# A hybrid-attention encoder layer on one core: sink logits as a score column, four rows normalized on ScalarE, one projection added by accumulating stores

## The chip, the cores and the metric

The kernel runs on one core of a Trainium2 chip. A core has TensorE (PE, matrix products into PSUM), VectorE (DVE), ScalarE (ACT) and GpSimd (POOL), and a queue on SyncE (SP) that issues DMA transfers; GpSimd issues transfers too. Each engine works through its own instructions in order and waits on semaphores for the others. The metric is the device time of one execution in microseconds, as a median over runs.

## The reference

One layer of a post-norm encoder on x of 1024 tokens by 1024 features, in float32:

```python
x = layer_norm(x, ln_in_g, ln_in_b)
proj = x @ w_in                                  # split into q, k, v of three groups
oa = neighbourhood_attention(...)                # A: 4 heads, 8x16 window on a 16x64 grid
ob = sliding_window_gqa(...)                     # B: 8 q heads, 2 kv heads, +-128 tokens, sinks
oc = differential_attention(...)                 # C: 4 heads, two softmaxes, full length
mix = concatenate([oa, ob, oc]) @ w_out
x = layer_norm(alpha * x + mix, ln_mix_g, ln_mix_b)
hdn = relu(x @ w_ff1)
x = layer_norm(alpha * x + (hdn * hdn) @ w_ff2, ln_ff_g, ln_ff_b)
```

In group B every query has one more logit, the sink of its head, which takes part in the softmax and has no value:

```python
sink_col = broadcast_to(sink, scores.shape[:-1] + (1,))
p = softmax(concatenate([scores, sink_col], axis=-1), axis=-1)[..., :-1]
```

## The kernel before

The 1024 tokens are eight tiles of 128. Products are made in two-part precision: each operand is split into a high part (a copy rounded to the matmul's type, on ScalarE) and a low part (a subtraction, L133, on VectorE or GpSimd), and `mm3` (L147) makes three products. Working tiles come from a pool of 36 pages of 4 KB per partition (`page`), and from small rings: `evb` has four buffers, PSUM has tags `S` (three banks), `mm` (two), `t` (two) and `pv` (one).

The program runs the input normalization and the first projections, then group C (steps 0 to 31 of one loop), group A (32 to 47), group B (48 to 63) with a few steps of lag for the values, and then the feed-forward layer, whose products (L930, L1044) fill TensorE to the end. Projections of later groups are put between as background work (`run_bg`). The order of instructions on each engine is set by a scheduler that simulates the program and follows priorities; `tc.high_priority(offset=...)` moves a block.

Group B is the third attention. One step `b_scores(i, g)` makes the scores of four heads for one tile of queries over up to three blocks of keys (n is 256 or 384 columns): for each head two matmuls (L720), one custom VectorE instruction (L722) that adds the position table, negates, writes the row to SBUF and gives the row's minimum against the negated sink, and one exponential on ScalarE (L725) whose accumulator gives the row's sum. Then four small instructions bring in the sinks: L728 adds sink and minimum (both in SBUF), L729 is its exponential, L730 adds the row sums (both in SBUF), L731 is the reciprocal. GpSimd multiplies the rows by it (L734). `b_values` transposes them (L746), splits them (L749, L133), multiplies by the values (L752) and splits the result (L755, L756, L761, L133 on 64x256).

`out_c(t)` makes group C's share of the output projection of tile t while groups A and B run, and stores its two halves to the DRAM tensor `y1c` from GpSimd's queue. `y1[t]` holds alpha times the normalized input, stored early. `out_ab(t, ob)` loads `y1[t]` and `y1c[t]` from SP's queue, adds them on GpSimd (L797), makes the shares of A and B (L147) and adds these on VectorE (L803). The eight results are normalized by `ln_mix_half`: statistics on VectorE (`ln_stats`, L210, L226, L228), a power on GpSimd (L229), the normalization itself on VectorE (L854), a store to `y2` from GpSimd's queue (L856), then transposes (L864) and splits. Half 0 (tiles 0 to 3) runs while group B still does, half 1 after it.

Of the kernel before, what the change touches and what calls it, by code (L numbers as in the profile page):

```python
# [13 lines left out]
AF = mybir.ActivationFunctionType  # L14
ALU = mybir.AluOpType
AX = mybir.AxisListType

P = 128
D = 1024
# [61 lines left out]
def encoder_kernel(ctx: ExitStack, tc: tile.TileContext, A: dict, out: bass.AP):  # L81
# [12 lines left out]
    def page(shape, dt=F32):  # L94
        return sb.tile(shape, dt, tag="pg", bufs=N_PG, name=nm("pg"))
# [25 lines left out]
    def dram(shape, name):  # L121
        return dr.tile(shape, F32, tag=name, bufs=1, name=name)
# [149 lines left out]
        return res  # L272

    y1 = [dram([P, D], f"y1_{t}") for t in range(NT)]
    y1c = dram([NT, P, D], "y1c")
    xT = [None, None]


# [429 lines left out]
    def b_scores(i, g, q, kk, tabs):  # L708
        k0, k1, off = b_range(i)
        n = (k1 - k0) * P  # L710
        sm = small([P, 4, 4], "bst")
        rts = []
        for h2 in range(2):
            rt = page([P, 2, 384])
            for j in range(2):
                hl = 2 * h2 + j
                sc = ps_s()
                h = 4 * g + hl
                for m in range(2):
                    nc.tensor.matmul(sc[:, 0:n], q[:, h, :], kk[g][m][:, k0 * P:k1 * P],  # L720
                                     start=(m == 0), stop=(m == 1))
                nc.vector.tensor_tensor_reduce(  # L722
                    out=rt[:, j, 0:n], in0=sc[:, 0:n], in1=tabs[h][:, off:off + n],
                    scale=-1.0, scalar=negsink[:, h:h + 1], op0=ALU.add, op1=ALU.min, accum_out=sm[:, 0, hl:hl + 1])
                nc.scalar.activation(out=rt[:, j, 0:n], in_=rt[:, j, 0:n], func=AF.Exp, scale=-1.0,  # L725
                                     bias=sm[:, 0, hl:hl + 1], accum_out=sm[:, 1, hl:hl + 1])
            rts.append(rt)
        nc.vector.tensor_tensor(out=sm[:, 2, :], in0=sink[:, 4 * g:4 * g + 4], in1=sm[:, 0, :], op=ALU.add)  # L728
        nc.scalar.activation(out=sm[:, 2, :], in_=sm[:, 2, :], func=AF.Exp)  # L729
        nc.vector.tensor_tensor(out=sm[:, 2, :], in0=sm[:, 2, :], in1=sm[:, 1, :], op=ALU.add)  # L730
        nc.vector.reciprocal(out=sm[:, 3, :], in_=sm[:, 2, :])  # L731
        for h2 in range(2):
            rt = rts[h2]
            nc.gpsimd.tensor_tensor(out=rt[:, :, 0:n], in0=rt[:, :, 0:n],  # L734
                                    in1=sm[:, 3, 2 * h2:2 * h2 + 2].unsqueeze(2).broadcast_to([P, 2, n]), op=ALU.mult)
        return rts
# [44 lines left out]
    def out_c(t):  # L781

        for nh in range(2):
            pm = ps_mm()
            sl = half_sl(nh)
            mm3(pm, [(*heads_of(t, n), w_o[6 + n][0][:, sl], w_o[6 + n][1][:, sl]) for n in range(2)])
            a_t = evb([P, 512])
            nc.scalar.copy(out=a_t, in_=pm)
            nc.gpsimd.dma_start(out=y1c[t, :, sl], in_=a_t)

    def out_ab(t, ob):

        a_t = page([P, D])
        load(out=a_t, in_=y1[t])
        c_t = page([P, D])
        load(out=c_t, in_=y1c[t])
        nc.gpsimd.tensor_tensor(out=a_t, in0=a_t, in1=c_t, op=ALU.add)  # L797
        for nh in range(2):
            pm = ps_mm()
            sl = half_sl(nh)  # L800
# [48 lines left out]
    def ln_mix_half(half):  # L849

        xs = fa[4 * half:4 * half + 4]
        for j in range(4):
            mean, rstd = ln_stats(xs[j])
            nc.vector.tensor_scalar(out=xs[j], in0=xs[j], scalar1=mean, scalar2=rstd,  # L854
                                    op0=ALU.subtract, op1=ALU.mult)
            nc.gpsimd.dma_start(out=y2[4 * half + j], in_=xs[j])  # L856
        if not ln_mix:
            ln_mix.append(ln_load("ln_mix"))
# [526 lines left out]
```

## Time and profile before

| what | us |
|---|---|
| median of 3 runs (1222.17 to 1224.81) | 1223.8 |
| the profiled execution | 1225.86 |
| its span in the profile | 1224.0 |
| TensorE, VectorE, ScalarE, GpSimd busy | 1148.0, 990.2, 642.9, 415.4 |

The span runs from the first to the last instruction of one profiled execution; times in the rows below count from its start. Busy time leaves out waits on semaphores, but not what an instruction waits for after it has begun. TensorE's ends are modelled, so its busy time is an upper figure. TensorE's mean granted clock is 0.98 of full speed.

### The profile page before, as it was taken

To read this page: it belongs to the slowest core of one execution; us is meant where nothing else is said; L and a number is where in the kernel's file an instruction comes from. 1 tells how busy PE (TensorE), PEld (TensorE's weight loads), DVE (VectorE), ACT (ScalarE), POOL (GpSimd) and SP (SyncE) were. 2 spreads that over 40 slices of the span, in tenths; PEclk is the share of its full clock that TensorE was granted. 3 is DMA by queue.
4 is the path that set the end of the run, shared out by engine and by line. 5 is a ranking of instruction groups with operands and counts; after the bars stand their busy time and mean duration, and the time that the engine had idled before them with its cause. 6 is when DMAs were issued, how large, how long until landed. Compare 5 with 4: busy or idle time off the path is not lost.

```text
span 1224.0 us, 17025 instructions
## 1 busy us (share of the span) xinstructions
PE 1148.0 (94%) x5642; PEld 949.4 (78%) x5642; DVE 990.2 (81%) x1886; ACT 642.9 (53%) x1239; POOL 415.4 (34%) x363
## 2 busy tenths in 40 slices
PE   4799999999998989988399999999999999999997
PEld 3578879987877867766288888888888888888886
DVE  7855899998666699986897698898684888777995
ACT  5323667766557876655655445455462444444440
POOL 5833556686576766531012122222120000000201
PEclk9889999999999999999599999999999999999999
DMA  7295835363789663324035575664389755255551
GB/s 237 104 303 162 276 127 167 121 166 123 209 228 303 199 164 104 104 86 155 26 129 180 175 244 191 225 230 154 141 318 346 250 178 190 103 187 189 183 163 69
DMA packets 127535, 220.59 MB, mean 180 GB/s; under 512 B 11404, under 2 KB 67628, under 8 KB 127448
## 3 DMA queue, kind: packets, MB, share of 16 engines
q1 hardware_dynamic: 113752, 173.36, 45.3%
q0 software_dynamic: 13696, 46.15, 9.9%
q8 instruction: 45, 0.74, 0.3%
q14 instruction: 42, 0.34, 0.1%
HBM read 152.30 MB, written 74.98 MB: 186 GB/s over the span
## 4 chain that ended last, share of the span: by engine, by line
PE 76%; DVE 12%; issue 5%; DMA 2%; ACT 2%; POOL 1%; SPq 0%; DVEq 0%; POOLq 0%; ACTq 0%
PE psm L147 15%; PE psS L1044 11%; PE psS L930 10%; PE pst L930 7%; PE psm L930 7%; PE pst L1044 5%; PE psm L1044 5%; PE pspv L1044 4%; PE psS L469 2%; PE pspv L513 2%; PE pst L498 2%; PE pst L147 2%; DVE pg L133 2%; DVE pg L238 2%; DVE pg L722 1%
## 5 line engine op out<-in xcount | busy, mean ns | idle before, releaser
L147 PE MATMUL psm<-pg,whi 128*128 128x512 f32 x448 | 150.0, 408 | 7.2 <-DVE pg L238 6.4
L930 PE MATMUL psS<-pg,pg 128*128 128x512 f32 x576 | 135.8, 393 | 9.1 <-ACT pg L827 9.1
L1044 PE MATMUL psS<-pg,pg 128*128 128x512 f32 x576 | 140.5, 389 | 0.0
L229 POOL TENSOR_TENSOR bnve<-bnve,pw 128x1 f32<-128x1 f32 x23 | 21.8, 954 | 335.9 <-DVE bnve L228 335.1
L930 PEld LDWEIGHTS psS<-pg,pg 128*128 128x128 f32 x576 | 109.4, 190 | 32.4 <-ACT pg L827 9.5
L1044 PEld LDWEIGHTS psS<-pg,pg 128*128 128x128 f32 x576 | 108.1, 188 | 22.4
L827 ACT CAST pg<-hr 128x512 fp32r<-128x512 f32 x112 | 69.3, 619 | 97.5 <-PE pst L1044 38.0
L147 PEld LDWEIGHTS psm<-pg,whi 128*128 128x128 f32 x448 | 84.0, 192 | 28.3 <-DVE pg L238 7.3
L476 ACT ACTIVATE pg<-pg,cst 128x1024 f32<-128x1024 f32 x64 | 73.8, 1153 | 57.7 <-DVE cst L472 52.1
L930 PE MATMUL psm<-pg,pg 128*128 128x512 f32 x384 | 89.8, 389 | 0.0
L930 PE MATMUL pst<-pg,pg 128*128 128x512 f32 x384 | 89.6, 389 | 0.0
L147 PE MATMUL psm<-pg,wlo 128*128 128x512 f32 x224 | 89.5, 401 | 0.1
L133 DVE TENSOR_TENSOR pg<-hr,pg 128x512 fp32r<-128x512 f32 x112 | 76.5, 683 | 13.2 <-ACT pg L827 13.1
L133 DVE TENSOR_TENSOR pg<-pst,pg 128x512 fp32r<-128x512 f32 (+2 forms) x112 | 64.5, 589 | 23.8 <-ACT pg L394 15.3
L930 PEld LDWEIGHTS psm<-pg,pg 128*128 128x128 f32 x384 | 72.1, 188 | 14.9
L930 PEld LDWEIGHTS pst<-pg,pg 128*128 128x128 f32 x384 | 72.1, 188 | 14.9
L147 PE MATMUL psm<-whi,pg 128*128 128x256 f32 (+1 forms) x256 | 72.7, 347 | 3.8 <-DVE pg L133 3.7
L938 POOL DMA_DIRECT2D hd<-h x32 | 17.7, 554 | 172.1 <-ACT h L942 172.1
L1044 PE MATMUL psm<-pg,pg 128*128 128x512 f32 x288 | 74.2, 389 | 0.0
L1044 PE MATMUL pst<-pg,pg 128*128 128x512 f32 x288 | 74.2, 389 | 0.0
L133 DVE TENSOR_TENSOR pg<-evb,pg 128x512 fp32r<-128x512 f32 (+1 forms) x112 | 72.7, 658 | 1.7 <-ACT pg L761 1.2
L941 ACT ACTIVATE h<-h 128x512 f32<-128x512 f32 x64 | 40.4, 632 | 62.6 <-DVE h L823 61.6
(214 smaller groups left out, 2818.1 us busy)
## 6 DMA issues: line engine op xcount, KB each, us to landing
hr<-hd SPq DMA_DIRECT2D x28, 1024.0 KB, 6.5
hd<-evb POOLq DMA_DIRECT2D x80, 256.0 KB, 3.2
w1r<-in_w_ff SPq DMA_DIRECT2D x16, 1024.0 KB, 6.1
evb<-in_w_ff SPq DMA_DIRECT2D x64, 256.0 KB, 3.6
qk<-evb SPq DMA_DIRECT2D x52, 256.0 KB, 2.4
y<-pg POOLq DMA_DIRECT2D x24, 512.0 KB, 3.4
pg<-y SPq DMA_DIRECT2D x24, 512.0 KB, 6.7
hd<-h POOLq DMA_DIRECT2D x32, 256.0 KB, 3.6
```

The lines of the kernel that those rows point to most:

```text
L133: nc.vector.tensor_tensor(out=o, in0=a, in1=b, op=ALU.subtract)
L147: nc.tensor.matmul(o, a, b, start=(i == 0), stop=(i == n - 1))
L229: nc.gpsimd.tensor_tensor(out=ve[:, 1:2], in0=ve[:, 0:1], in1=pw[:, 0:1], op=ALU.pow)
L238: last_sub[0] = eng.tensor_tensor(out=xp[:, 1, :], in0=tmp, in1=f32(xp[:, 0, :]), op=ALU.subtract)
L469: last_mm[0] = nc.tensor.matmul(sc, q[:, m, (i % 2) * P:(i % 2) * P + P], kst[h][kh][:, m, :], start=True, stop=True)
L476: nc.scalar.activation(out=rt, in_=rt, func=AF.Exp, scale=-1.0, bias=sm[:, m:m + 1], accum_out=sm[:, 2 + m:3 + m])
L498: nc.tensor.transpose(pt[:, kb * P:(kb + 1) * P], src[:, c0:c0 + P], ident)
L513: nc.tensor.matmul(pv[:, 0:256], Vc[h // 2][kb // 4][:, kb % 4, h % 2, :], src[:, kb % 4, :], start=(n == 0), stop=(n == 15))
L827: nc.scalar.copy(out=pg[:, 0], in_=x)
L930: nc.tensor.matmul(o, w[:, e, k], xo[m][k][:, f], start=(n == 0), stop=(n == 11))
L941: nc.scalar.activation(out=dst, in_=dst, func=AF.Relu)
L1044: nc.tensor.matmul(o, h[:, e, sl], w[:, f], start=(k == 0 and n == 0), stop=(k == 15 and n == 2))
```

## The change

Three edits. In `b_scores` a page has rows of 386 columns; ScalarE copies the negated sinks of two heads into column n, the exponential runs over n + 1 columns, so that its accumulator holds the whole denominator, and L728, L729 and L730 are gone. In `ln_mix_half` the first half's four tiles are normalized by one ScalarE instruction each, with a scale of 1/std and a bias of minus mean times 1/std, which a new VectorE instruction makes. In `out_c` the two stores of a tile go onto `y1[t]` with addition in the DMA, and `out_ab` loads `y1[t]` alone; the second load, its page and GpSimd's addition are gone, and `y1c` too.

```diff
--- before.py
+++ after.py
@@ -272,7 +272,6 @@
         return res
 
     y1 = [dram([P, D], f"y1_{t}") for t in range(NT)]
-    y1c = dram([NT, P, D], "y1c")
     xT = [None, None]
 
 
@@ -711,7 +710,10 @@
         sm = small([P, 4, 4], "bst")
         rts = []
         for h2 in range(2):
-            rt = page([P, 2, 384])
+            rt = page([P, 2, 386])
+
+            h = 4 * g + 2 * h2
+            nc.scalar.copy(out=rt[:, :, n:n + 1], in_=negsink[:, h:h + 2].unsqueeze(2))
             for j in range(2):
                 hl = 2 * h2 + j
                 sc = ps_s()
@@ -722,13 +724,10 @@
                 nc.vector.tensor_tensor_reduce(
                     out=rt[:, j, 0:n], in0=sc[:, 0:n], in1=tabs[h][:, off:off + n],
                     scale=-1.0, scalar=negsink[:, h:h + 1], op0=ALU.add, op1=ALU.min, accum_out=sm[:, 0, hl:hl + 1])
-                nc.scalar.activation(out=rt[:, j, 0:n], in_=rt[:, j, 0:n], func=AF.Exp, scale=-1.0,
+                nc.scalar.activation(out=rt[:, j, 0:n + 1], in_=rt[:, j, 0:n + 1], func=AF.Exp, scale=-1.0,
                                      bias=sm[:, 0, hl:hl + 1], accum_out=sm[:, 1, hl:hl + 1])
             rts.append(rt)
-        nc.vector.tensor_tensor(out=sm[:, 2, :], in0=sink[:, 4 * g:4 * g + 4], in1=sm[:, 0, :], op=ALU.add)
-        nc.scalar.activation(out=sm[:, 2, :], in_=sm[:, 2, :], func=AF.Exp)
-        nc.vector.tensor_tensor(out=sm[:, 2, :], in0=sm[:, 2, :], in1=sm[:, 1, :], op=ALU.add)
-        nc.vector.reciprocal(out=sm[:, 3, :], in_=sm[:, 2, :])
+        nc.vector.reciprocal(out=sm[:, 3, :], in_=sm[:, 1, :])
         for h2 in range(2):
             rt = rts[h2]
             nc.gpsimd.tensor_tensor(out=rt[:, :, 0:n], in0=rt[:, :, 0:n],
@@ -786,15 +785,12 @@
             mm3(pm, [(*heads_of(t, n), w_o[6 + n][0][:, sl], w_o[6 + n][1][:, sl]) for n in range(2)])
             a_t = evb([P, 512])
             nc.scalar.copy(out=a_t, in_=pm)
-            nc.gpsimd.dma_start(out=y1c[t, :, sl], in_=a_t)
+            nc.gpsimd.dma_start(out=y1[t][:, sl], in_=a_t, accum_op=ALU.add)
 
     def out_ab(t, ob):
 
         a_t = page([P, D])
         load(out=a_t, in_=y1[t])
-        c_t = page([P, D])
-        load(out=c_t, in_=y1c[t])
-        nc.gpsimd.tensor_tensor(out=a_t, in0=a_t, in1=c_t, op=ALU.add)
         for nh in range(2):
             pm = ps_mm()
             sl = half_sl(nh)
@@ -851,8 +847,13 @@
         xs = fa[4 * half:4 * half + 4]
         for j in range(4):
             mean, rstd = ln_stats(xs[j])
-            nc.vector.tensor_scalar(out=xs[j], in0=xs[j], scalar1=mean, scalar2=rstd,
-                                    op0=ALU.subtract, op1=ALU.mult)
+            if half == 0:
+                nmr = small([P, 1], "nmr", 2)
+                nc.vector.scalar_tensor_tensor(out=nmr, in0=mean, scalar=-1.0, in1=rstd, op0=ALU.mult, op1=ALU.mult)
+                nc.scalar.activation(out=xs[j], in_=xs[j], func=AF.Identity, scale=rstd, bias=nmr)
+            else:
+                nc.vector.tensor_scalar(out=xs[j], in0=xs[j], scalar1=mean, scalar2=rstd,
+                                        op0=ALU.subtract, op1=ALU.mult)
             nc.gpsimd.dma_start(out=y2[4 * half + j], in_=xs[j])
         if not ln_mix:
             ln_mix.append(ln_load("ln_mix"))
```

Line numbers of the changed kernel differ by a few from those before: L716 is the copy of the sinks, L724 the custom instruction, L727 the exponential, L730 the reciprocal, L733 GpSimd's multiplication, L799 the addition of the output product, L852 and L853 the new pair of the normalization, L857 the store to `y2`.

On GpSimd, around the moment when the first tiles are normalized (L229 is the power for a tile's standard deviation), before:

```order
L734 TENSOR_TENSOR pg_5000<-pg_5000,bst_4988 128x768
L229 TENSOR_TENSOR bnve_5974<-bnve_5974,pw 128x1
L797 TENSOR_TENSOR pg_5129<-pg_5129,pg_5131 128x1024
L856 DMA y_0_108<-pg_4940 128x1024
L734 TENSOR_TENSOR pg_5060<-pg_5060,bst_5059 128x768
L734 TENSOR_TENSOR pg_5071<-pg_5071,bst_5059 128x768
L734 TENSOR_TENSOR pg_5178<-pg_5178,bst_5177 128x768
L734 TENSOR_TENSOR pg_5189<-pg_5189,bst_5177 128x768
L797 TENSOR_TENSOR pg_5318<-pg_5318,pg_5320 128x1024
```

and now:

```order
L733 TENSOR_TENSOR pg_4991<-pg_4991,bst_4978 128x2x384
L229 TENSOR_TENSOR bnve_5939<-bnve_5939,pw 128x1
L857 DMA y_0_107<-pg_4933 128x1024
L733 TENSOR_TENSOR pg_5049<-pg_5049,bst_5048 128x2x384
L733 TENSOR_TENSOR pg_5061<-pg_5061,bst_5048 128x2x384
L733 TENSOR_TENSOR pg_5163<-pg_5163,bst_5162 128x2x384
L733 TENSOR_TENSOR pg_5175<-pg_5175,bst_5162 128x2x384
L229 TENSOR_TENSOR bnve_5951<-bnve_5951,pw 128x1
L733 TENSOR_TENSOR pg_5233<-pg_5233,bst_5232 128x2x384
```

The addition of `y1` and `y1c` (L797) no longer stands behind the power; the store of the normalized tile (now L857, which waits for ScalarE) and the multiplications of the scores follow it at once.

On VectorE, at the normalization of tile 0, before:

```order
L722 ISA pg_5178,bst_5177<-psS_5179,pg_4032,negsink 128x384
L722 ISA bst_5177 128x1
L722 ISA pg_5178,bst_5177<-psS_5184,pg_4032,negsink 128x384
L722 ISA bst_5177 128x1
L728 TENSOR_TENSOR bst_5059<-sink,bst_5059 128x4
L854 TENSOR_SCALAR pg_4940<-pg_4940,bnmv_5972,bnve_5974 128x1024
L756 TENSOR_TENSOR evb_5122<-pspv_5088,evb_5122 64x512
L722 ISA pg_5189,bst_5177<-psS_5190,pg_4081,negsink 128x384
L722 ISA bst_5177 128x1
L722 ISA pg_5189,bst_5177<-psS_5195,pg_4081,negsink 128x384
L722 ISA bst_5177 128x1
L730 TENSOR_TENSOR bst_5059<-bst_5059 128x4
```

and now:

```order
L133 TENSOR_TENSOR pg_5006<-evb_5041,pg_5006 64x256
L228 TENSOR_SCALAR bnve_5939<-bnmv_5937 128x1
L133 TENSOR_TENSOR pg_5006<-evb_5041,pg_5006 64x256
L133 TENSOR_TENSOR ev_5105<-pst_5099,ev_5104 128x512
L852 SCALAR_TENSOR_TENSOR nmr_5942<-bnmv_5937,bnve_5939 128x1
L724 ISA pg_5061,bst_5048<-psS_5068,pg_4367,negsink 128x384
L724 ISA bst_5048 128x1
L133 TENSOR_TENSOR ev_5198<-pst_5192,ev_5197 128x512
L724 ISA pg_5163,bst_5162<-psS_5165,pg_4031,negsink 128x384
L724 ISA bst_5162 128x1
L724 ISA pg_5163,bst_5162<-psS_5170,pg_4031,negsink 128x384
L724 ISA bst_5162 128x1
```

The additions L728 and L730 and the normalization L854 are gone from VectorE; the one new instruction is L852 on one column, which comes after the power on GpSimd.

On ScalarE, inside the steps of scores of one tile, before:

```order
L725 ACTIVATE pg_5260,bst_5248<-pg_5260,bst_5248 128x384
L749 CAST ev_5402<-pst_5397 128x512
L725 ACTIVATE pg_5260,bst_5248<-pg_5260,bst_5248 128x384
L725 ACTIVATE pg_5367,bst_5366<-pg_5367,bst_5366 128x384 x2
L729 ACTIVATE bst_5248<-bst_5248 128x4
L755 COPY evb_5311<-pspv_5277 64x512
L749 CAST ev_5413<-pst_5408 128x512
L725 ACTIVATE pg_5378,bst_5366<-pg_5378,bst_5366 128x384
L761 CAST pg_5206<-evb_5311 64x256 x2
```

and now:

```order
L853 ACTIVATE pg_5117<-pg_5117,nmr_5954,bnve_5951 128x1024
L727 ACTIVATE pg_5347,bst_5346<-pg_5347,bst_5346 128x385
L754 COPY evb_5294<-pspv_5260 64x512
L748 CAST ev_5392<-pst_5387 128x512
L727 ACTIVATE pg_5359,bst_5346<-pg_5359,bst_5346 128x385 x2
L760 CAST pg_5190<-evb_5294 64x256 x2
L748 CAST ev_5403<-pst_5398 128x512
L748 CAST ev_5450<-pst_5445 128x512
L754 COPY evb_5409<-pspv_5375 64x512
L748 CAST ev_5461<-pst_5456 128x512
L760 CAST pg_5374<-evb_5409 64x256 x2
L716 COPY pg_5417<-negsink 128x2
```

The exponential of four columns (L729) is gone; a normalization (L853, tile 1) stands between two exponentials, ahead of the copy and the casts of the values; and four copies of the sinks, of which the first is shown, stand ahead of the exponentials of the next two steps, each the first writer of its page.

## Rows read from the trace of the kernel before

**Rows 1.** Stretches: start:end, length; PE, PEld, DVE, ACT, POOL busy (xcount); PEclk, DMA, GB/s.

```profile
431.00:543.00 112.00, 102.73 (x508) 80.90 (x507) 108.25 (x251) 70.76 (x190) 62.49 (x46) 0.98 0.41 125
...
583.00:611.00 28.00, 8.06 (x32) 5.88 (x31) 25.45 (x43) 18.89 (x32) 2.07 (x3) 0.57 0.07 28
611.00:1224.00 613.00, 605.32 (x2664) 500.86 (x2662) 494.42 (x783) 275.74 (x475) 76.23 (x127) 0.99 0.56 192
```

**Rows 2.** Timeline of PE, 431 to 543, rows after a wait: start, us, instructions [idle before].

```profile
439.06 1.16 PE L720 MATMUL psS<-pg,pg 128*128 128x384 f32 x4 [1.55 <-DVE bst L722]
...
450.59 0.73 PE L147 MATMUL psm<-whi,pg 128*128 128x512 f32 x2 [1.32 <-DVE pg L133]
...
488.27 0.73 PE L147 MATMUL psm<-whi,pg 128*128 128x512 f32 x2 [1.11 <-DVE pg L133]
...
525.30 0.73 PE L147 MATMUL psm<-whi,pg 128*128 128x512 f32 x2 [1.24 <-DVE pg L133]
...
537.53 0.63 PE L746 MATMUL pst<-ident,pg 128*128 128x128 f32 x4 [0.93 <-DVE bst L728]
...
539.07 1.97 PE L752 MATMUL pspv<-ev,pg 128*128 128x512 f32 x4 [0.91 <-DVE evb L756]
```

**Rows 3.** Groups of DVE by shape, 431 to 543: xcount | busy us, mean ns | idle before.

```profile
L133 DVE TENSOR_TENSOR pg<-evb,pg 64x256 fp32r<-64x256 f32 x24 | 15.8, 659 | 0.8 <-ACT pg L761 0.4
L854 DVE TENSOR_SCALAR pg<-pg,bnmv,bnve 128x1024 f32<-128x1024 f32 x5 | 9.9, 1978 | 0.1
L728 DVE TENSOR_TENSOR bst<-sink,bst 128x4 f32<-128x4 f32 x13 | 8.1, 626 | 0.1
...
L730 DVE TENSOR_TENSOR bst<-bst 128x4 f32<-128x4 f32 x13 | 5.1, 390 | 0.4 <-ACT bst L729 0.3
```

**Rows 4.** Timeline of DVE and POOL at four places of the third attention.

```profile
447.51 2.55 POOL L797 TENSOR_TENSOR pg<-pg,pg 128x1024 f32<-128x1024 f32 x1
...
448.30 1.78 DVE L728 TENSOR_TENSOR bst<-sink,bst 128x4 f32<-128x4 f32 x1
...
481.60 0.80 DVE L854 TENSOR_SCALAR pg<-pg,bnmv,bnve 128x1024 f32<-128x1024 f32 x1
...
496.41 2.39 POOL L797 TENSOR_TENSOR pg<-pg,pg 128x1024 f32<-128x1024 f32 x1
...
496.65 2.71 DVE L854 TENSOR_SCALAR pg<-pg,bnmv,bnve 128x1024 f32<-128x1024 f32 x1
...
533.50 2.88 DVE L854 TENSOR_SCALAR pg<-pg,bnmv,bnve 128x1024 f32<-128x1024 f32 x1
```

**Rows 5.** PE in 431:543 of L147, L752, L720, L746 alone; two pieces of the chain.

```profile
431.00:543.00 112.00, 53.22 (x201) 36.03 (x199) 0.98 0.41 125
431.00:543.00 112.00, 24.36 (x69) 12.95 (x70) 0.98 0.41 125
431.00:543.00 112.00, 23.78 (x98) 16.10 (x98) 0.98 0.41 125
431.00:543.00 112.00, 19.82 (x136) 16.38 (x136) 0.98 0.41 125
...
472.54 0.87 PE pst L746 x8
473.41 2.79 PE psm L147 x12
```

**Rows 6.** The line L789: issue ns min/median/max, first and last start; landing.

```profile
L789 POOL DMA_DIRECT2D y1c<-evb x16: 539/580/641, 389.2 to 431.4; - x16
...
DMA to landing us min/median/max: 2.3/4.5/6.1
```

**Rows 7.** ACT: the line L250 (min/median/max ns), and L729 by shape in 431:543.

```profile
L250 ACT ACTIVATE pg<-pg,nmr,bnve x2: 1224/1226/1227, 9.3 to 10.4; 128x1024 f32<-128x1024 f32 x2
...
L729 ACT ACTIVATE bst<-bst 128x4 f32<-128x4 f32 x13 | 2.6, 200 | 4.5 <-DVE bst L728 4.4
```

**Rows 8.** Timeline of DVE at the last tile's addition.

```profile
582.18 0.69 DVE L803 TENSOR_TENSOR pg<-pg,psm 128x512 f32<-128x512 f32 x1 [4.47 <-POOL pg L797]
```

## The prediction

> **What bounds the kernel now.** I read the stretches first [rows 1]. From 611 us on TensorE is busy for 605 of 613 us, so nothing in the two feed-forward stages can get shorter unless they begin sooner; the stretch ahead of them (583 to 611) has TensorE idle for 20 of its 28 us and waits on one serial chain, the second half's normalization, its transposes and the splits that VectorE makes. This chain begins when the last tile's output product is done. The question is therefore by how much the change brings that moment forward. In the third attention, 431 to 543, VectorE is busy for 108.2 of 112.0 us and ScalarE for 70.8; TensorE shows 102.7, so 9.3 us of visible idleness. All its waits there end on VectorE; the six longest stand in [rows 2] (1.55, 1.32, 1.11, 1.24, 0.93, 0.91 us), and VectorE is what to look at.
>
> VectorE is not short of arithmetic there. The rows by shape [rows 3] show a 128x4 addition that takes 626 ns on the mean (L728), another that takes 390 (L730), and a normalization of 128x1024 that takes 1978 (L854). Beside GpSimd's rows [rows 4] one sees why: an addition of four columns that starts at 448.30 inside GpSimd's 2.55 us addition of 447.51 ends 1.78 later, when that one ends; the normalization takes 0.80 alone (481.60), but 2.71 when it starts 0.24 behind GpSimd's add (496.65), and 2.88 at 533.50. A VectorE instruction that reads two SBUF tensors, or this normalization, stands still until GpSimd's instruction is over, and everything behind it on VectorE, and the matmuls that need it, stand too.
>
> **The change, part by part.**
>
> *Sinks.* In this stretch 13 of the 16 L728 (8.1 us in sum) and 13 of the 16 L730 (5.1) go [rows 3]; most of these 13.2 us are holds. A hold is gained only where the next VectorE instruction isn't one that would be held as well; mostly it is a row minimum (L722), which reads PSUM and one SBUF tensor. ScalarE loses 13 exponentials of 0.20 us [rows 7] and gets 26 copies of two columns. No such copy is in the trace; its cost lies between 0 and the 0.20 of the 128x4 exponential, and I take the 0.20, since both are nearly all fixed cost. The exponential grows by one column of 384, which is nothing. The normalization on GpSimd now runs on rows of 386 pitch; the shape with 256 columns has always run with gaps, so I take no change there.
>
> *Normalization of tiles 0 to 3.* Five L854 make 9.9 us in the stretch; the last (2.88, tile 4) stays, so 7.0 us leave VectorE. ScalarE gets four ACTIVATEs of this shape at 1.23 us each [rows 7], 4.9 us. Four new 128x1 VectorE instructions read two SBUF tensors; they cost between 0 and the 0.39 of L730, I take 0.2 each, 0.8 in all. [...]
>
> *C's part.* Eight GpSimd additions of 2.4 us go, and with them eight loads of 512 KB and their pages. What they held on VectorE goes too: tile 4's L854 falls from 2.88 to 0.80 [rows 4], 2.1 us. At the end VectorE waits 4.47 us for the last of these additions [rows 8], but TensorE works until 583 on the same tile's product, so the gain at that place lies between 0 and 4.5 and I take 0.3, nearest to the lower end. Sixteen stores become accumulating ones. The trace has only plain ones, 0.58 us to issue and 4.5 to land [rows 6]; an accumulating one costs at least that (below that nothing speaks for a gain), at most perhaps three times as much to land, since it must also read its target. I take up to twice, 9 us. It is hidden by the ring of four evb buffers: 16 stores in the 42.2 us from 389.2 to 431.4 are one per 2.64 us, so a buffer may be held for 10.6 us; issue 0.6, a copy taken to be as long, and landing 9 make 10.2. Without that cover each extra microsecond of landing costs 16/4 = 4 us.
>
> *Sum.* VectorE loses 13.2 + 7.0 + 2.1 - 0.8 = 21.5 us and falls from 108.2 to about 87. TensorE's own work in the stretch [rows 5] is 270 matmuls of 512 columns at 2.79/12 = 0.2325, 98 of 384 at three quarters of that (0.174), and 136 transposes at 0.87/8 = 0.109: 62.8 + 17.1 + 14.8 = 94.7 us. So TensorE becomes the floor, and no more than 112.0 - 94.7 = 17.3 us is there to be had: 9.3 visible and 8.0 that the modelled ends cover. Of the visible waits 439.06 and 450.59 sit behind a held L728, 537.53 and 539.07 behind the held L854: 4.7 us that go. Those at 488.27 and 525.30 follow splits of 64x256 that read two SBUF tensors and stand behind GpSimd's own normalizations of the scores; they stay (2.35). Of the other 2.2 I take 1.3, between 0 and 2.2. Visible gain 6.0, two thirds of it all. If the covered part shrinks in the same share, 8.0 x 0.65 = 5.2 more; if not at all, nothing. The middle is 6.0 + 2.6 = 8.6. Add 0.3 at the end, and take off 0.9 for ScalarE, whose new work is 26 x 0.20 - 2.6 + 4.9 = 7.5 us on an engine with 41 us free: bounds 0 and 7.5, near the lower end because TensorE doesn't wait for ScalarE in this stretch today. Result: 8.0 us. The profiled execution took 1225.86 us (span 1224.0), so 1217.9; the median of the runs shown is 1223.8, and 2.1 us less, so **1215.8**. About 0.2% (2.4 us) is what a measurement tells from no change.
>
> **Rivals.**
>
> *A, the holds move.* The 24 splits of 64x256 (659 ns on the mean [rows 3]) and the four new 128x1 instructions still read two SBUF tensors, and GpSimd still makes its normalizations of the scores. Each of the four stands in VectorE's queue behind the power that GpSimd makes for it, and GpSimd may go on at once with the next tile's scores, as it did with the addition of 496.41. Two or three holds of 1.5 to 1.9 us, say 5 us, come back: 1223.8 - 3.0 = 1220.8. [...] Against it: on GpSimd the first of the four is followed by the store of the same tile, which waits itself, and the scores that follow the other three may not be ready yet. Chance 0.17.
>
> *B, ScalarE becomes the engine that is waited for.* The normalization (1.23) and the copies, which may wait for a free page, stand in its queue ahead of the casts that TensorE needs. All 7.5 us in the way: gain 8.6 + 0.3 - 7.5 = 1.4, so 1222.4. Against it: 37% of it is idle. Chance 0.08.
>
> *C, slower.* If accumulating stores land late, TensorE waits in the stretch ahead (389 to 431) for ScalarE's copy, which waits for an evb buffer. The loss is 16 x ((landing + 1.2)/4 - 2.64): none up to 9.4 us, 8.0 at 11.4, where the gain is used up. At 13.5, three times today's, it is 16.6: 1215.8 + 16.6 = 1232.4. For it: the store reads and writes, nothing in the trace bounds it. [...] Chance 0.11.
>
> *D, VectorE is no longer waited for at all.* TensorE then runs near its floor: 9.3 visible and 5.2 covered, with the same 0.6 off: 13.9 us, 1209.9. Against it: the splits behind GpSimd's normalizations. Chance 0.14.
>
> **How the numbers follow.** The forecast has 0.50, by itself 1212 to 1219.5. The range 1208.5 to 1224.5 takes in D, A and B, and leaves C and the far ends out. Faster by over 0.2% are the forecast, D, most of A (0.12) and half of B (0.04): 0.80. Within 0.2%: the rest of A and B (0.09). Slower: C, 0.11.
>
> **What would show it.** Right: the stage of steady TensorE begins near 603, not 611; VectorE's row of 128x4 additions is gone and its busy time between the start of the third attention and its end is near 87 us; tile 4's L854 takes 0.8; the last tile's addition waits for TensorE, not for GpSimd. Wrong: waits of TensorE on ScalarE's copies in 389 to 431 with a landing over 9 us (C); the new 128x1 instructions with a mean over 1 us (A); TensorE's waits in the third attention ending on ScalarE (B). A fall of TensorE's granted clock that the change moves would upset the sum as well; it is 0.98 in the stretch now [rows 1].

## The result, and the profile after

The changed kernel takes 1215.66 us (median of 4 runs, 1213.73 to 1219.53) against 1224.3 for the kernel before: a ratio of 0.9936, with a 95% interval of 0.9908 to 0.9965. In a second set of runs it was 0.9934 (0.9914 to 0.9953). The prediction was 1215.8. The profiled execution is the slowest of the first four, 1219.53 us, with a span of 1217.7.

The stretches of [rows 1], now; the columns are the same, from the length to GB/s:

```profile
431.00:543.00 112.00, 107.84 (x554) 87.67 (x552) 98.53 (x238) 81.73 (x217) 53.26 (x43) 1.00 0.33 92
583.00:611.00 28.00, 12.29 (x40) 9.76 (x41) 27.59 (x46) 18.95 (x34) 0.00 (x0) 0.54 0.00 0
611.00:1224.00 613.00, 598.58 (x2641) 495.47 (x2639) 486.80 (x771) 273.31 (x469) 76.40 (x127) 0.99 0.56 192
```

In the same 112 us TensorE does 554 matmuls where it did 508, with 4.2 us of visible idleness where it had 9.3, and VectorE is busy for 98.5 where it was for 108.2, although the stretch now holds more of the work. The part of steady TensorE begins at 602.65 instead of 610.39.

TensorE's timeline, 431 to 543, of the rows after a wait the four longest, in order of time (start, us; in brackets the idle time before and what ended it):

```profile
434.43 0.73 PE L147 MATMUL psm<-hd,pg 128*128 128x512 f32 x2 [0.84 <-DVE pg L133]
437.34 0.63 PE L745 MATMUL pst<-ident,pg 128*128 128x128 f32 x4 [0.68 <-DVE ev L133]
443.64 0.61 PE L722 MATMUL psS<-pg,pg 128*128 128x384 f32 x2 [0.72 <-DVE bst L724]
...
532.24 1.19 PE L751 MATMUL pspv<-ev,pg 128*128 128x512 f32 x4 [0.52 <-DVE evb L755]
```

The longest wait is 0.84 us; in [rows 2] six were between 0.91 and 1.55. The groups of VectorE by shape in the same stretch (xcount | busy us, mean ns | idle before) show that VectorE now waits for TensorE, 5.2 us in its custom instructions and 2.5 in the additions of the output product:

```profile
L724 DVE CUSTOM_DVE_ANT_0 pg<-psS,pg,negsink 128x384 f32<-128x384 f32 x44 | 25.4, 606 | 5.5 <-PE psS L722 5.2
...
L133 DVE TENSOR_TENSOR pg<-evb,pg 64x256 fp32r<-64x256 f32 x26 | 17.0, 655 | 0.8
...
L799 DVE TENSOR_TENSOR pg<-pg,psm 128x512 f32<-128x512 f32 x12 | 8.1, 676 | 2.5 <-PE psm L147 2.5
...
L855 DVE TENSOR_SCALAR pg<-pg,bnmv,bnve 128x1024 f32<-128x1024 f32 x2 | 1.6, 812 | 0.7 <-POOL bnve L229 0.7
...
L852 DVE SCALAR_TENSOR_TENSOR nmr<-bnmv,bnve 128x1 f32<-128x1 f32 x4 | 0.6, 150 | 0.0
```

The additions of [rows 3] are gone, no normalization is held any more (0.81 us), the new 128x1 instruction takes 150 ns at each of its four places, and the splits of 64x256 are as slow as before (655 ns, 659 in [rows 3]). Single lines: the accumulating stores, the copies of the sinks and the normalization on ScalarE (ns min/median/max, first and last start), and VectorE at the last tile's addition:

```profile
L788 POOL DMA_DIRECT2D y<-evb x16: 850/990/1836, 390.5 to 432.8; - x16
...
DMA to landing us min/median/max: 4.7/5.1/7.1
...
L716 ACT COPY pg<-negsink x32: 182/189/205, 408.2 to 524.8; 128x2 f32<-128x2 f32 x32
...
L853 ACT ACTIVATE pg<-pg,nmr,bnve x4: 1231/1234/1246, 460.9 to 514.6; 128x1024 f32<-128x1024 f32 x4
...
574.51 0.69 DVE L799 TENSOR_TENSOR pg<-pg,psm 128x512 f32<-128x512 f32 x1 [4.34 <-PE psm L147]
```

A store takes 0.99 us to issue (0.58 in [rows 6]) and lands after 5.1 (4.5), at most 7.1, and no wait in the profile ends on it. The last addition waits for TensorE, not for GpSimd [rows 8].

### The profile page after: what moved, and what is told of

Read it like the earlier page. It is cut to its first block, busy times and chain, and to the rows that moved or that the text cites. A ratio compares the mean times of both kernels' runs of the same rounds, so it can differ in the third digit from the quotient of the medians.

```text
span 1217.7 us, 16999 instructions
## 1 busy us (share of the span) xinstructions
PE 1145.6 (94%) x5642; PEld 950.5 (78%) x5642; DVE 968.2 (80%) x1854; ACT 649.6 (53%) x1259; POOL 401.1 (33%) x355
## 4 chain that ended last, share of the span: by engine, by line
PE 82%; DVE 11%; ACT 3%; issue 2%; DMA 1%; SPq 1%; POOL 0%; DVEq 0%; ACTq 0%; POOLq 0%
PE psm L147 18%; PE psS L931 11%; PE psS L1045 11%; PE pst L931 7%; PE psm L931 7%; PE psm L1045 5%; PE pst L1045 5%; PE pspv L1045 4%; DVE pg L133 2%; PE pst L147 2%; PE psS L468 2%; PE pspv L512 2%; PE pst L497 2%; DVE pg L238 2%; DVE pg L471 1%
## 5 line engine op out<-in xcount | busy, mean ns | idle before, releaser
L147 PE MATMUL psm<-pg,whi 128*128 128x512 f32 x448 | 150.0, 408 | 7.3 <-DVE pg L238 6.4
L229 POOL TENSOR_TENSOR bnve<-bnve,pw 128x1 f32<-128x1 f32 x23 | 21.6, 943 | 364.4 <-DVE bnve L228 362.9
L147 PEld LDWEIGHTS psm<-pg,whi 128*128 128x128 f32 x448 | 84.0, 192 | 28.2 <-DVE pg L238 7.3
L147 PE MATMUL psm<-pg,wlo 128*128 128x512 f32 x224 | 89.4, 401 | 0.1
L931 PEld LDWEIGHTS psm<-pg,pg 128*128 128x128 f32 x384 | 72.1, 188 | 14.9
L931 PEld LDWEIGHTS pst<-pg,pg 128*128 128x128 f32 x384 | 72.1, 188 | 14.9
L147 PE MATMUL psm<-whi,pg 128*128 128x256 f32 (+1 forms) x256 | 72.2, 345 | 0.7 <-DVE pg L133 0.5
```

The source lines that it names most:

```text
L147: nc.tensor.matmul(o, a, b, start=(i == 0), stop=(i == n - 1))
L229: nc.gpsimd.tensor_tensor(out=ve[:, 1:2], in0=ve[:, 0:1], in1=pw[:, 0:1], op=ALU.pow)
L931: nc.tensor.matmul(o, w[:, e, k], xo[m][k][:, f], start=(n == 0), stop=(n == 11))
```

## The experiments

The theory: the 128x4 additions, the splits of 64x256 and the normalizations stand still on VectorE while a tensor instruction of GpSimd runs (L728 1.78 us at 448.30, L854 2.71 at 496.65 [rows 4]), so VectorE's time is set by who meets whom, and the three edits free partly the same time. First rival: VectorE's instructions count with their own time, held or not. Second rival: each edit works by itself and the parts add up. All ratios are against the kernel before on the same chip, 5 to 12 runs each; "VectorE" is its busy time in the whole profile, and "stage" the time in the profile from the first custom instruction of the third attention's scores to the start of the last tile's addition [rows 8]. A gain in the text is the ratio's distance from 1, times 1225 us. Line numbers shift by a few from kernel to kernel. Every edit lets the scheduler order the instructions anew, and the stage of the changed kernel differs by 1.1 us between two profiles with the same order (in one of them the granted clock was 0.50 from 547.25 to 550.66, in the other not), so a difference of 1 us between two kernels is not read.

| kernel | median us | ratio (95%) | VectorE | stage |
|---|---|---|---|---|
| before | 1224.3 to 1225.7 | 1 | 990.2 | 175.2 |
| sinks alone | 1217.46 | 0.9941 (0.9922 to 0.9961) | 981.2 | 168.9 |
| normalization alone | 1224.01 | 0.9999 (0.9985 to 1.0012) | 986.1 | 173.9 |
| stores alone | 1219.78 | 0.9955 (0.9938 to 0.9973) | 980.5 | 167.6 |
| sinks, normalization | 1216.07 | 0.9937 (0.9923 to 0.9952) | 971.4 | 165.4 |
| sinks, stores | 1215.06 | 0.9927 (0.9915 to 0.9939) | 970.9 | 163.2 |
| all three | 1217.55 | 0.9934 (0.9914 to 0.9953) | 968.2, 969.1 | 166.2, 165.1 |
| + 64 additions | 1226.23 | 1.0012 (1.0000 to 1.0025) | 989.9 | 175.7 |
| + 64 multiplications | 1225.69 | 1.0020 (1.0002 to 1.0038) | 988.6 | 173.9 |
| + 64 reciprocals | 1217.49 | 0.9946 (0.9926 to 0.9967) | 974.7 | 166.8 |
| before, no L734 | 1220.15 | 0.9969 (0.9953 to 0.9985) | 983.0 | 170.4 |
| sinks, stores, 58 idle matmuls | 1213.36 | 0.9917 (0.9896 to 0.9938) | 965.7 | 163.7 |
| sinks, stores, 84 idle matmuls | 1211.42 | 0.9887 (0.9869 to 0.9905) | 966.3 | 164.4 |

**The sinks alone.** The hunks of `b_scores`, on the kernel before:

```diff
+            nc.scalar.copy(out=rt[:, :, n:n + 1], in_=negsink[:, h:h + 2].unsqueeze(2))
...
-        nc.vector.tensor_tensor(out=sm[:, 2, :], in0=sink[:, 4 * g:4 * g + 4], in1=sm[:, 0, :], op=ALU.add)
-        nc.scalar.activation(out=sm[:, 2, :], in_=sm[:, 2, :], func=AF.Exp)
-        nc.vector.tensor_tensor(out=sm[:, 2, :], in0=sm[:, 2, :], in1=sm[:, 1, :], op=ALU.add)
```

> The sinks' edit alone on the kernel before; GpSimd's additions L797, VectorE's normalizations and the plain stores stay. Theory of holds: the 26 additions L728 and L730 cost 13.2 us of VectorE in the third attention, of which 26 x 0.16 = 4.2 are their own time and some 9 are waits behind GpSimd. All of it goes; at the ratio that the prediction's sum gave (8.6 us of 21.5, 0.4) this is 5.3 us, so about 1218.5 to 1219.5. Rival, instructions count and holds don't: only the 4.2 us go, 1.7 us at the same ratio, about 1222.5. Rival, the holds move to the splits of 64x256, which read two SBUF tensors: their mean rises from 659 ns to 900 or more, and the gain is under 2 us.

It gains 7.2 us, more than expected. VectorE loses 9.0 us and not 13.2. The same view by shape shows why:

```profile
L133 DVE TENSOR_TENSOR pg<-evb,pg 64x256 fp32r<-64x256 f32 x26 | 16.3, 626 | 0.5
L854 DVE TENSOR_SCALAR pg<-pg,bnmv,bnve 128x1024 f32<-128x1024 f32 x6 | 13.7, 2289 | 0.7 <-POOL bnve L229 0.7
```

The holds don't move to the splits (626 ns), but to the normalizations, which now take 2289 ns on the mean instead of 1978.

**The normalization alone.** The hunk of `ln_mix_half`:

```diff
+            if half == 0:
+                nmr = small([P, 1], "nmr", 2)
...
+                nc.scalar.activation(out=xs[j], in_=xs[j], func=AF.Identity, scale=rstd, bias=nmr)
```

> The normalization of tiles 0 to 3 on ScalarE alone. Theory of holds: VectorE loses 4 instructions of 7.0 us in sum, of which 3.8 are two holds behind L797, and gets 0.6; but L797 is still there and finds other instructions to hold: a gain of 1 to 2.5 us, 1222 to 1223. Rival, by free prices (0.80 on VectorE against 1.23 on ScalarE): no gain, 1224 to 1226.

Nothing is gained, and the median lies where the rival put it. Four instructions of 7 us leave VectorE, but it gets only 4.1 us shorter: L728 is held longer, 732 ns on the mean instead of 626, tile 4's normalization still takes 2.9 us, and the new 128x1 instruction is held itself, once for 2204 ns inside L797 (the other three take at most 159):

```profile
L728 DVE TENSOR_TENSOR bst<-sink,bst 128x4 f32<-128x4 f32 x13 | 9.5, 732 | 0.0
...
L859 DVE TENSOR_SCALAR pg<-pg,bnmv,bnve 128x1024 f32<-128x1024 f32 x1 | 2.9, 2875 | 0.1
...
L856 DVE SCALAR_TENSOR_TENSOR nmr<-bnmv,bnve 128x1 f32<-128x1 f32 x4 | 2.7, 666 | 0.1
```

**The stores alone.** The hunks of `out_c` and `out_ab`:

```diff
-            nc.gpsimd.dma_start(out=y1c[t, :, sl], in_=a_t)
+            nc.gpsimd.dma_start(out=y1[t][:, sl], in_=a_t, accum_op=ALU.add)
...
-        nc.gpsimd.tensor_tensor(out=a_t, in0=a_t, in1=c_t, op=ALU.add)
```

> The accumulating stores alone, with L797, its loads and pages gone; VectorE's arithmetic is unchanged. Theory of holds: in the third attention 8.2 us of VectorE's time are waits behind L797 (three L854 5.9, one L728 1.6, one split 0.7); they go, 3.3 us at the ratio 0.4 and 0.3 at the end, about 1220.5; the longest L854 is then 1 us or less. Rival, instructions count: VectorE does as much as before, so 0 to 0.3 us, about 1224. Rival, the stores cost: slower than before.

It gains 5.5 us. Not one VectorE instruction is taken away here (1886 in both profiles), and VectorE is busy for 9.7 us less: as an account of VectorE's time the first rival is refuted. Most of it is in the normalization's line, 0.81 us at each of six places where five took 1.98 on the mean [rows 3]. How much of the 5.5 us comes from the loads and pages that go too, this run alone doesn't tell. The profile's busy times before and here, and the normalization here:

```profile
PE 1148.0 (94%) x5642; PEld 949.4 (78%) x5642; DVE 990.2 (81%) x1886; ACT 642.9 (53%) x1239; POOL 415.4 (34%) x363
...
PE 1148.5 (94%) x5642; PEld 952.6 (78%) x5642; DVE 980.5 (80%) x1886; ACT 643.6 (53%) x1239; POOL 400.0 (33%) x355
...
L850 DVE TENSOR_SCALAR pg<-pg,bnmv,bnve 128x1024 f32<-128x1024 f32 x6 | 4.8, 808 | 0.7 <-POOL bnve L229 0.7
```

**All three again.** The changed kernel, beside its parts.

> The changed kernel once more beside its parts on the same chip: a ratio of 0.9935 (0.992 to 0.995). If the theory of holds is right the three parts alone add to more than this (0.4 x (13.2 + 6.4 + 8.2) = 11 us against 8), because two edits free the same holds: L854 behind L797. If the parts are independent they add to it.

The parts alone make 7.2 + 0.1 + 5.5 = 12.8 us, together they make 8.1: the second rival is refuted as well, for the kernel's time (resampled from the runs, the difference lies between 2 and 8 us). But the profiles don't show the edits freeing the same VectorE time: alone they take 9.0 + 4.1 + 9.7 = 22.8 us off VectorE, together 22.0 and 21.1. VectorE's parts nearly add up, and less of the sum becomes kernel time.

**Two at a time.** The changed kernel with the plain stores put back, and the changed kernel with all normalizations on VectorE. The second one's edit:

```diff
-            if half == 0:
...
-            else:
-                nc.vector.tensor_scalar(out=xs[j], in0=xs[j], scalar1=mean, scalar2=rstd,
+            nc.vector.tensor_scalar(out=xs[j], in0=xs[j], scalar1=mean, scalar2=rstd,
```

> The changed kernel with the stores put back (plain stores to y1c, its load and GpSimd's addition L797). Theory of holds: with the sinks' edit the normalizations were held longest (six L854 of 2.29 us); on ScalarE they are not, so the stage is 0 to 2 us shorter than with the sinks alone; and the feed-forward part, which took 614.6 to 615.1 us in the three profiles with accumulating stores and 613.2 to 613.6 in the three without, takes 613.4: 1215.5 to 1217, no slower than the changed kernel. Rival, the three edits help independently: the stores' part of 5.5 us is missing, 1222.

> The changed kernel without the normalization on ScalarE (sinks and stores only). Theory of holds: with L797 gone the normalization takes 0.8 on VectorE, so four of them cost 3.2 - 0.6 = 2.6 us of an engine that now waits for TensorE; 1217 to 1218.5, not to be told from the changed kernel (1217.5). Rival, each edit adds its own part: 2 us or more slower, 1219.5 to 1220.5.

Both are as fast as the changed kernel within the intervals. Sinks and normalization take 18.8 us off VectorE, where alone they take 9.0 and 4.1: the holds that each leaves to the other's instructions go with both. Sinks and stores take off 19.3, about the sum of theirs. Without the stores' edit the normalization on ScalarE makes the stage 3.5 us shorter in the profiles (168.9 to 165.4), though the medians hardly show it; with it, it brings nothing that is measured (0.9934 against 0.9927; the stage 165.1 and 166.2 against 163.2). In the kernel without it VectorE's rows are

```profile
L133 DVE TENSOR_TENSOR pg<-evb,pg 64x256 fp32r<-64x256 f32 x26 | 14.7, 564 | 0.4
L850 DVE TENSOR_SCALAR pg<-pg,bnmv,bnve 128x1024 f32<-128x1024 f32 x6 | 4.8, 807 | 0.7 <-POOL bnve L229 0.7
```

The normalization takes its free 0.81 there, and the splits 564 ns instead of 655. A side expectation of the first run fell: its feed-forward part takes 614.3 us with plain stores, not 613.4, so that part's length doesn't go with the stores alone (the last two runs take this up).

**Held or counted.** In the changed kernel one small instruction more behind each of the 64 custom instructions, on constants, so that it waits for no engine. The three kernels differ in this line only. By the profiles the first two have the same order on all engines, but for one of the new instructions at the program's start; in the third some fifty places of VectorE's order differ:

```diff
+                nc.vector.tensor_tensor(out=sm[:, 2, :], in0=sink[:, 4 * g:4 * g + 4], in1=negsink[:, 4 * g:4 * g + 4], op=ALU.add)
```

```diff
+                nc.vector.tensor_scalar(out=sm[:, 2, :], in0=sink[:, 4 * g:4 * g + 4], scalar1=-1.0, scalar2=None, op0=ALU.mult)
```

```diff
+                nc.vector.reciprocal(out=sm[:, 2, :], in_=sink[:, 4 * g:4 * g + 4])
```

> The changed kernel with one VectorE addition of 128x4 more behind each of the 64 custom instructions of the scores; both operands are constants in SBUF, so it waits for no engine, and its result is not used. Theory of holds: GpSimd is at tensor work for nearly half of this stage, so an addition meets it about every second time and stands still for some 0.45 us on the mean: 0.6 us each, 39 us in all; VectorE's 110 us in the 134 from 411 to 545 would be 149, so the stage grows by 15 us or more: 1228 to 1242. Rival, only arithmetic counts: 64 x 0.16 = 10 us, VectorE stays below the stage's length, 1218 to 1221.

> The same as the run with the additions, with the same order of instructions on every engine, but each of the 64 is a multiplication of one SBUF tensor of 128x4 by a constant. Theory of holds, if only a second SBUF operand makes an instruction wait for GpSimd: 0.15 us each, 10 us, 1218 to 1221, some 10 us or more below the additions. If the one-input form is held as well (as the normalization of 128x1024, which has one tensor operand, was): as slow as the additions. Rival, only arithmetic counts: both runs alike, within 1 us of each other, 1218 to 1221.

> The changed kernel with 64 reciprocals of 128x4 more, one behind each custom instruction of the scores, where the runs before had additions (0.42 us each) or multiplications by a constant (0.41). Reciprocals are the only small instruction of which no row is longer than 0.18 us. Theory of holds: 64 x 0.17 = 11 us on VectorE, each 0.17 us at every place, and 3 to 7 us below the two runs with the same number of instructions: 1218.5 to 1222. Rival, the number of instructions counts (each one delays the queue, held or not): 1225 to 1226.5 like the other two.

The additions take back the whole gain, the multiplications too, and the reciprocals nothing that is measured (1217.49, the changed kernel 1217.55). The groups of the new line in the three kernels, VectorE by shape from 405 to 560 (60 of the 64; the scheduler put four to the program's start):

```profile
L727 DVE TENSOR_TENSOR bst<-sink,negsink 128x4 f32<-128x4 f32 x60 | 24.8, 416 | 0.6
```

```profile
L727 DVE TENSOR_SCALAR bst<-sink 128x4 f32<-128x4 f32 x60 | 24.3, 408 | 0.6
```

```profile
L727 DVE RECIPROCAL bst<-sink 128x4 f32<-128x4 f32 x60 | 9.9, 170 | 0.5
```

Equal counts and equal data, 170 ns against 408 and 416; all three take 160 to 172 ns in their medians, so the difference is a few long rows. Ten of the 60 additions take 0.8 to 5.9 us, and each of these ends with an instruction of GpSimd (six with the scores' multiplication, four with L163, a subtraction that splits weights); the other fifty stay under 0.2. Of the 60 reciprocals 23 begin and end while GpSimd is at a tensor instruction, and none takes over 0.18. This was the decisive run for the first rival. The additions cost less than I expected (0.42 instead of 0.6 us each, 1226 instead of 1228 or more): ten of 60 were held, not every second one. And the multiplication with one tensor operand is held like the addition with two, so two SBUF operands are not the condition.

**The holder taken away.** The kernel before, without GpSimd's multiplications:

```diff
-            nc.gpsimd.tensor_tensor(out=rt[:, :, 0:n], in0=rt[:, :, 0:n],
-                                    in1=sm[:, 3, 2 * h2:2 * h2 + 2].unsqueeze(2).broadcast_to([P, 2, n]), op=ALU.mult)
```

> The kernel before without GpSimd's multiplications L734, so the division of the scores by the softmax's sum is left out; VectorE has the same instructions as before. Theory of holds: in the third attention 11.8 us of VectorE's time are waits behind L734 (splits 6.2, L730 3.1, L728 2.5); with these gone and L797 still there the gain is 5 to 9 us, 1216 to 1220, and the splits of 64x256 take 0.55 us or less on the mean (0.66 before), L730 0.17. Rival, VectorE's arithmetic is what counts: 1223.5 to 1225.5.

The gain is 3.8 us where the theory expected 5 at the least; the median is 0.15 us above its range and 3.4 below the rival's. The scores no longer wait for GpSimd either, so the gain needn't be all VectorE's. The splits are free, as expected. The rest is still held: the normalization takes 2372 ns, behind L797, and L730 262 where 170 was expected (1.15 us at one place behind L797, 0.56 at another behind L163):

```profile
L850 DVE TENSOR_SCALAR pg<-pg,bnmv,bnve 128x1024 f32<-128x1024 f32 x5 | 11.9, 2372 | 0.1
L133 DVE TENSOR_TENSOR pg<-evb,pg 64x256 fp32r<-64x256 f32 x26 | 10.8, 417 | 0.8 <-ACT pg L757 0.4
...
L730 DVE TENSOR_TENSOR bst<-bst 128x4 f32<-128x4 f32 x13 | 3.4, 262 | 0.4 <-ACT bst L729 0.3
```

**The clock at the start of the feed-forward part.** This part took 613.2 to 615.1 us in the profiles so far, 613.6 before, 615.1 and 614.6 in the two of the changed kernel. The stretches from its first matmul, in the kernel before and in the changed one, show TensorE at a granted clock of 0.50 for some 4 and some 6 us:

```profile
610.39:613.39 3.00, 3.00 (x7) 2.38 (x8) 2.93 (x6) 0.47 (x1) 0.00 (x0) 0.50 0.01 3
613.39:616.39 3.00, 3.00 (x12) 2.40 (x12) 2.97 (x6) 2.48 (x5) 0.00 (x0) 0.85 0.00 0
```

```profile
602.65:605.65 3.00, 3.00 (x7) 2.38 (x8) 2.93 (x6) 0.47 (x1) 0.00 (x0) 0.50 0.00 0
605.65:608.65 3.00, 3.00 (x8) 2.32 (x8) 2.97 (x6) 2.49 (x5) 0.00 (x0) 0.50 0.00 0
```

Two runs put matmuls whose result nobody reads into TensorE's idle places ahead of this part, in the kernel with sinks and stores only: 10, 8, 8, 8 and 24 behind the last products and behind each piece of the second half's transposes, and then 14, 8, 12, 16 and 34.

```diff
+    def warm(n):
+        pm = ps_pv()
+        with tc.issue_after(last_pe[0].ins):
+            for i in range(n):
+                last_pe[0] = nc.tensor.matmul(pm, xo[1][0][:, 0, 0:P], xo[1][0][:, 0], start=True, stop=True)
```

> The sinks and the stores without the normalization on ScalarE (1215.1 in its own run), and 58 matmuls of 512 columns, whose result is not used, in TensorE's idle places between the last product and the feed-forward part. In all profiles so far the granted clock fell in this place and came back 3.0 to 6.0 us after the first steady matmul, and the feed-forward part took 613.2 us where it came back after 3.0 and 615.1 where after 6.0. Theory, the part's length is set by that return: with TensorE busy the clock is 1.00 when the steady part begins, and the part takes 611.7 to 612: 1212.5 to 1214. Rival, the part differs for another cause (the order of its instructions): 613 to 615 as before, 1215 or more, and later by what the idle matmuls delay.

> The run with idle matmuls, with more of them (84 instead of 58): there TensorE still waited 1.2, 1.2, 2.4 and 2.6 us between them, the granted clock was 0.50 twice, the second time from 1 us before to 3 us behind the first steady matmul, and the feed-forward part took 613.9 us. Now the waits are some 0.3 us each. Theory, the clock's fall follows TensorE's idle places and its return sets the part's length: 1.00 throughout, the part takes 612.0 to 612.4, 1211 to 1213. Rival, the clock falls here whatever TensorE does, or the part's length has another cause: 613.3 to 614, 1213 to 1215.

In the first the clock fell later, but it did fall and was low once more where the part begins, so it tells neither from the other. In the second the clock is 1.00 all through. From 570 on, the first run's stretches and the second's:

```profile
570.00:590.00 20.00, 15.17 (x73) 11.56 (x73) 14.93 (x26) 10.69 (x19) 2.07 (x3) 1.00 0.11 42
590.00:598.00 8.00, 7.99 (x32) 6.36 (x31) 7.79 (x13) 5.03 (x9) 0.00 (x0) 0.79 0.00 0
598.00:604.00 6.00, 3.36 (x9) 2.45 (x8) 5.93 (x11) 3.39 (x7) 0.00 (x0) 0.74 0.00 0
```

```profile
570.00:590.00 20.00, 18.80 (x93) 14.53 (x92) 17.06 (x29) 11.26 (x19) 2.06 (x3) 1.00 0.10 39
590.00:598.00 8.00, 6.68 (x30) 5.20 (x28) 7.90 (x14) 6.52 (x12) 0.00 (x0) 1.00 0.00 0
598.00:604.00 6.00, 5.09 (x21) 3.78 (x22) 5.90 (x10) 2.95 (x7) 0.00 (x0) 1.00 0.01 3
```

So in these two profiles the low clock goes with TensorE's idle places (waits of 1.2, 3.6 and 2.6 us in sum in the first run, 0.3, 0.9 and 2.0 in the second). The part takes 612.9 us, between the two expectations. The starts of its matmuls in the traces show where its length differs. The first 24 take 6.16 us here, 7.0 to 7.4 where the clock came back after 3.0 to 3.9 us, and 8.4 where it came back after 6.0. From there to the last matmul's start all 14 profiles take 598.17 us. Behind that start stand 8.1 us in the five profiles with plain stores and 8.5 in the nine with accumulating ones, for a cause that was not looked for. So the clock's return sets the length at the front, and the stores' edit adds 0.5 us at the end. The kernel takes 1211.42 us, 0.9887 of the kernel before, and its interval lies below those of the changed kernel and of sinks and stores alone. Of the 3.6 us between it and the latter the profiles' feed-forward parts show 0.9 (613.8 to 612.9). Where the rest is stays open, for these profiles can't show it: the one is of the slowest execution of its kernel (1213.33), the other of the fastest (1214.08).

## Why the prediction was right, point by point

**The bound.** VectorE was the engine to look at, and its time was mostly holds: shown by the stores alone (9.7 us off, no instruction less) and by the reciprocals beside the additions. What was wrong is the condition, "a VectorE instruction that reads two SBUF tensors, or this normalization": a multiplication of 128x4 by a constant is held as well (408 ns on the mean, 164 in the median), a reciprocal is not (170, at most 180), nor is the 128x1 L228, of one operand, which in the kernel before took 132 ns at 17.86, inside GpSimd's subtractions L351 of 13.78 to 18.89. What sets the held forms apart from the others, no run here shows.

The list of holders was too short as well. The longest L728 stands behind neither L797 nor L734, but behind L163:

```profile
436.08 2.36 POOL L163 TENSOR_TENSOR pg<-pg,pg 128x1024 fp32r<-128x1024 f32 x1 [4.14 <-ACT pg L161]
...
436.43 2.03 DVE L728 TENSOR_TENSOR bst<-sink,bst 128x4 f32<-128x4 f32 x1
```

Of the time that L728 is held in the third attention some 3.3 us are L163's, 1.8 L797's and 1.3 L734's; the change leaves L163 as it is. And the wait at 488.27, which the prediction booked behind a split and left in, has a held L728 before it too (486.34, 1.42 us).

**The sum of VectorE.** 21.5 us were to go from the stretch; from the whole profile 22.0 and 21.1 went (990.2 to 968.2 and 969.1). "About 87" was a poor sign to name, for the stretch from 431 to 543 now holds more of the work.

**The shares.** Here the working failed, though the sum held. Holds were booked with the held instruction, and they belong as much to the holder. C's part was given 2.1 us of VectorE and 0.3 at the end; alone it frees 9.7 and gains 5.5, since three of the normalization's holds (5.9 us less in its line [rows 3, 4]) and some of L728's were L797's doing. The normalization on ScalarE was given 7.0 us; alone it gains nothing, and beside the other two nothing that is measured. The step that failed is to book the normalizations at the times of the kernel before (2.71 at 496.65): these rows hold only while L797 is there, and the same change takes it away. Then 0.81 us on VectorE stands against 1.23 on ScalarE, and to leave the normalization on VectorE is no loss (sinks and stores alone, 0.9927). The sinks' 13.2 us were right as a sum of rows, but alone 9.0 went.

**The floor and the gain.** At the slots of [rows 5] the 112 us now hold 308 matmuls of 512 columns, 98 of 384 and 137 transposes, counted in the second profile: 71.6 + 17.1 + 14.9 = 103.6 us, so of the 17.3 that were there 8.4 are left. Visible idleness fell by 5.1 (6.0 forecast). The stage got 9.0 and 10.1 us shorter in the two profiles, so the covered part gave 4 to 5 instead of 2.6. Three things that the sum did not have took some of it back. The feed-forward part's first 24 matmuls took 1.0 and 0.5 longer, where the clock came back after 6.0 and 4.9 us instead of 3.9; its end took 0.5 longer; and the stage began 1.3 and 1.2 later, for an open cause. So the spans got 6.3 and 8.0 us shorter. That 8.0 were forecast and 8.1 measured is errors that cancel: luck, to that digit. VectorE's time and the gain don't go together far: 9.0 us less gain 7.2 (sinks alone) and 9.7 gain 5.5 (stores alone), but 15.5 gain 6.6 (the reciprocals), 18.8 gain 7.7, 19.3 gain 8.9 and 22.0 gain 8.1, each by some 2 us either way. With the first 9 or 10 us most of the gain is made; in the changed kernel VectorE waits for TensorE, as its groups above show.

**Small terms.** The sinks' copies take 189 ns (200 taken), the 128x1 instructions 150 (200), the normalization on ScalarE 1.23 (1.23). GpSimd's multiplications take 1590 and 1376 ns in the second profile (384 and 256 columns, 405 to 545) after 1478 and 1038; no change was assumed, and the cause was not tried.

**The rivals.** A: the new instruction is not held (at most 153 ns in both profiles) and the splits are no slower, so with all three edits the holds don't move. No tensor instruction of GpSimd ran at its eight places, and where L797 is kept it was held, for 2204 ns with the normalization alone and 1345 with sinks and normalization. With the normalization alone the holds move (L728 732 ns), as they do with the sinks alone (L854 2289). B: of TensorE's waits of 431 to 543 none ends on ScalarE, and over the whole stage these are some 2 us, as before; the 0.9 taken off for ScalarE is not seen. C: the stores land in 7.1 us at most, and no wait ends on them; twice and three times a plain store's landing were estimates, the median is 5.1 against 4.5. D: in part; waits on VectorE are shorter, not gone.

## What to carry to other kernels

Where an instruction takes far longer in some places than in others, find the instruction of the other engine that ends with it, and price the removal of the holder beside that of the held: eight additions on GpSimd were worth 5.5 us, four held normalizations alone nothing, since other instructions were held in their stead. Edits that touch the same waits are to be priced together, in the kernel that the others leave behind; a row of the kernel before is no price once its cause is gone. And time taken off one engine is kernel time only as far as the next one has room: 22.8 us off VectorE, part by part, would be 12.8 of gain, and the three together gave 8.1. Forms that are not held (a reciprocal here, 170 ns) cost only their own time.

## What was not expected of the hardware

A VectorE multiplication of 128x4 by a constant, with one SBUF operand, was held by GpSimd like an addition of two (408 and 416 ns on the mean, 164 and 160 in the median), and 64 of them cost 8 us by the medians. One addition of 128x4 stood for 5.87 us, over two of GpSimd's multiplications, a store's issue and a subtraction. An accumulating store of 256 KB from GpSimd's queue took 0.99 us to issue and 5.1 to land, beside 0.58 and 4.5 for a plain one. The granted clock came back 3 to 6 us after TensorE's steady work began, differently in profiles of the same stage, and with 84 matmuls in the idle places it stayed at 1.00 there; 598.17 of the part's 613 us were the same in all 14 profiles.
